# A chunk-state scan put wholly on VectorE and spread over more turns, its output stage packed into fewer

## The chip, the cores and the metric

The kernel runs on one core of a Trainium2 chip. The core has five engines with a queue of instructions each: TensorE (PE in the rows, its weight loads PEld), VectorE (DVE), ScalarE (ACT), GpSimd (POOL) and SyncE (SP), which here only issues DMA transfers. The metric is the device time of one execution in microseconds; several executions are timed and the median is taken.

## The reference

One decoder layer works on x of 1024 tokens by 2048 channels, in float32. A normed x goes through one projection of 2048 by 4096 columns, whose parts are a pooling branch, its gate, a state-space branch `u` and its gate. The state-space branch is what the change touches: 64 groups of 16 channels, each with a complex state of 64, and a linear recurrence over time.

```
bu = einsum(u, bb)                       # per group
s[t] = a * s[t-1] + bu[t]                # complex, associative scan over 1024 tokens
y = Re(c s) + d * u
g = gelu(y)
hg = g @ w_glu
yb = hg[:, :1024] * sigmoid(hg[:, 1024:]) * silu(ssm_gate)
h = x + concat(ya, yb) @ w_out           # ya: pooling branch
out = rmsnorm(h + (p @ w_ple) * sigmoid(h @ w_ple_gate))
```

GELU is computed as y * sigmoid(c0 * (y + 0.044715 y^3)) with c0 = 1.5958.

## The kernel before, in words

The program is a list of **steps**. Nearly all of them are matmul steps of the large projections. One step of the input projection is 12 matmuls of 128x512: two weight blocks, three products each (every float32 weight and input is split into two fp32r parts, and hi*hi, hi*lo and lo*hi are taken), for both halves of the tokens. Before a step runs, its weight block, loaded from HBM into a tile `raw`, is split: ACT casts it into the first half of a tile `w` (L210), DVE subtracts to get the second half (L99, `w<-raw,w`). `emit(s)` writes these splits up to `SA = 4` steps ahead of the matmuls, and there are six `w` tiles. After the last step of a block of eight, a "gate post" reads two finished PSUM banks: two multiplies of 128x512 on DVE, two sigmoids on ACT, two more multiplies on DVE.

**Turns.** The state-space branch is a Python generator, `ssm()`, that is advanced in the background: `emit` calls `next` on it once for each 2.56 us of nominal matmul time, which for the steps here is once per step. What the generator issues up to its next `yield` is one turn. So a turn lies between two groups of 12 matmuls, on every engine in program order, and an extra `yield` moves all later state-space work one step of 12 matmuls on.

The branch works on chunks of T = 8 tokens, NC = 128 chunks. Its stages around the change:

- `ss_v`: per turn eight small matmuls give chunk inputs, copied by ACT and DVE into two tiles `V` of 64 chunks each (128 partitions x 64 chunks x 64).
- `ss_scan`: the recurrence over chunks. First eight *bulks*: each multiplies the states of the eight even chunks of 16 by the complex factor AR, AI and adds them to the odd ones, four `tensor_tensor` operations of 128x512 (`t<-V,AR`, `t<-V,AI`, `V<-V,t` twice). Then 63 sequential steps over the odd chunks, each four operations of 128x64 on DVE (`tA`, `tB`, `V`, `V`), two steps per turn. After every eighth step one more bulk fills the even chunks of the 16 just passed. Before, the bulks of odd j in the first stage and all of the second stage are on POOL.
- `ss_y`: for each of 16 sets of four groups (g0), 16 small matmuls (L1005 on `ytm`, `yu`; L1007 on `yl`, `ys`; each stands as several rows), then the GELU, then a store. `shift(g0 + 4)` copies the states for the next set out of V (four ACT and four DVE copies), `mask_t` makes `ytm` from the loaded `yt` on POOL, `ld(g0 + 8)` loads `yt`, `yu` and `yl`, 256 KB each. The first two turns of `ss_y` are taken early, inside the scan.

The scan's stage lies between the last small matmul of `ss_v` and the first of `ss_y`; PE meanwhile runs input-projection steps. The GELU result goes to `g_d` in HBM, and is loaded again (`gt`) by steps that have a fixed place in the list.

Of the kernel before, what the change touches and what calls it, by code (L numbers as in the profile page):

```python
# [11 lines left out]
AF = mybir.ActivationFunctionType  # L12
ALU = mybir.AluOpType
# [3 lines left out]
P = 128  # L17
# [22 lines left out]
def hybrid_trunk(ctx: ExitStack, tc: tile.TileContext, x, p, norm_gain, w_in, w_pool, pool_scale,  # L40
# [4 lines left out]
    dve = nc.vector  # L45
    act = nc.scalar
    pool = nc.gpsimd
# [4 lines left out]
    out = out[0]  # L52
# [33 lines left out]
    def st(dt=F32, shape=(P, HT), name="st"):  # L86
        return st_p.tile(list(shape), dt, tag="st", name=name)
# [4 lines left out]
    def aux(name="aux"):  # L92
        return aux_p.tile([P, HT], F32, tag="aux", name=name)
# [4 lines left out]
    def tt(eng, o, a, b, op):  # L98
        eng.tensor_tensor(out=o, in0=a, in1=b, op=op)  # L99

    def ts(eng, o, a, s1, op0, s2=None, op1=None):
        if op1 is None:
            eng.tensor_scalar(out=o, in0=a, scalar1=s1, scalar2=None, op0=op0)
        else:
            eng.tensor_scalar(out=o, in0=a, scalar1=s1, scalar2=s2, op0=op0, op1=op1)

    def stt(o, a, s, b, op0, op1):
        dve.scalar_tensor_tensor(out=o, in0=a, scalar=s, in1=b, op0=op0, op1=op1)
# [16 lines left out]
    AR = cst.tile([P, 64], F32, name="AR")  # L125
# [47 lines left out]
    def store(o, i, n=1):  # L173

        late.append([n, o, i])
# [359 lines left out]
    for h in range(2):  # L535
        for c0 in range(0, KD, 4):
# [7 lines left out]
            for kk, mb in chs:  # L544
                k = c0 + kk
# [31 lines left out]
    def both(*gens):  # L577
        gens = list(gens)
        while gens:
            gens = [g for g in gens if next(g, "end") != "end"]  # L580
            yield
# [276 lines left out]
    V = {}  # L858

    def u_rows(dst, g0):  # L860
        sp.dma_start(out=dst.rearrange("p (g k) -> p g k", g=4),
                     in_=u_d.rearrange("(g c) t k -> (c t) g k", c=C)[:, g0:g0 + 4])
# [39 lines left out]
    def cmul(eng, cur, prev, ar, ai, t1, t2):  # L902

        tt(eng, t1, prev, ar, ALU.mult)
        n = len(prev.shape)
        a, b = ("p (r c) -> p r c", 1) if n == 2 else ("p k (r c) -> p k r c", 2)
        sw = prev.rearrange(a, r=2)
        sw = sw[:, ::-1] if n == 2 else sw[:, :, ::-1]
        tt(eng, t2.rearrange(a, r=2), sw, ai.rearrange(a, r=2), ALU.mult)
        tt(eng, cur, cur, t1, ALU.add)  # L910
        tt(eng, cur, cur, t2, ALU.add)

    def bulk(eng, cur, prev):
        n = cur.shape[1]
        t1 = st(name="t1")[:, 0:n * 64].rearrange("p (k c) -> p k c", c=64)
        t2 = st(name="t2")[:, 0:n * 64].rearrange("p (k c) -> p k c", c=64)
        cmul(eng, cur, prev, AR.unsqueeze(1).to_broadcast([P, n, 64]),
             AI.unsqueeze(1).to_broadcast([P, n, 64]), t1, t2)

    def ss_scan():  # L920

        for j in range(8):
            v = V[j // 4][:, (j % 4) * 16:(j % 4) * 16 + 16]
            bulk(pool if j % 2 else dve, v[:, 1::2], v[:, 0::2])
            yield
        yield
        for k in range(3, NC, 2):
            prev = V[(k - 2) // 64][:, (k - 2) % 64]
            cur = V[k // 64][:, k % 64]
            cmul(dve, cur, prev, AR2, AI2, tA, tB)  # L930
            if k % 16 == 15:
                a = k - 15
                v = V[a // 64]
                a %= 64
                if a:
                    bulk(pool, v[:, a:a + 16:2], v[:, a - 1:a + 14:2])
                else:
                    bulk(pool, v[:, 2:16:2], v[:, 1:14:2])
                    if k > 64:
                        bulk(pool, v[:, 0:1], V[0][:, 63:64])  # L940
            if k % 4 == 3:
                yield
        yield

    def ss_y():
        tiles = {}

        def ld(g0):
            if g0 >= G:
                return  # L950
            ttl, ut, lt = (st(name=nm) for nm in ("yt", "yu", "yl"))

            kr = K_d[g0 * C * P:]
            sp.dma_start(out=ttl.rearrange("p (g m) -> p g m", g=4),
                         in_=bass.AP(tensor=kr.tensor, offset=kr.offset,
                                     ap=[[C, P], [C * P, 4], [1, P]]))
            u_rows(ut, g0)
            sp.dma_start(out=lt.rearrange("p (g m) -> p g m", g=4), in_=L_d[:, g0:g0 + 4])
            tiles[g0] = [lt, ttl, ut]

        def mask_t(g0):
            if g0 >= G:
                return
            tm = st(name="ytm")
            tt(pool, tm.rearrange("p (g c i) -> p g i c", g=4, i=T),
               tiles[g0][1].rearrange("p (g i c) -> p g i c", g=4, i=T),
               mask.unsqueeze(1).unsqueeze(3).to_broadcast([P, 4, T, C]), ALU.mult)
            tiles[g0][1] = tm

        def shift(g0):  # L970
            if g0 >= G:
                return
            sv = st(name="ys")
            tiles[g0].append(sv)
            sv = sv.rearrange("p (c e k) -> p e c k", c=2, e=2)
            c = g0 // 2
            n = 0
            for e in range(2):
                dve.memset(sv[:, e, :, 0:1], 0.0)
                for r in range(2):  # L980
                    for hf in range(2):
                        w = 64 - hf
                        o = sv[r * 64:r * 64 + 64, e, :, hf * 64 + 1:hf * 64 + 1 + w]
                        i = V[hf][e * 64:e * 64 + 64, 0:w, r * 32 + c:r * 32 + c + 2]
                        i = i.rearrange("p k c -> p c k")
                        if n % 2:
                            dve.tensor_copy(out=o, in_=i)
                        else:
                            act.copy(out=o, in_=i)
                        n += 1  # L990

        ld(0)
        yield
        mask_t(0)
        ld(4)
        yield
        shift(0)
        yield
        c0 = 1.5957691216057308
        for g0 in range(0, G, 4):  # L1000
            lt, ttl, ut, sv = tiles.pop(g0)
            b = aux()
            for i in range(4):
                o = b[:, i * P:(i + 1) * P]
                pe.matmul(out=o, lhsT=ttl[:, i * P:(i + 1) * P], rhs=ut[:, i * P:(i + 1) * P],  # L1005
                          start=True, stop=False)
                pe.matmul(out=o, lhsT=lt[:, i * P:(i + 1) * P], rhs=sv[:, i * P:(i + 1) * P],  # L1007
                          start=False, stop=True)
            del lt, ttl, ut, sv
            shift(g0 + 4)  # L1010
            q = st(name="yq")
            act.activation(out=q, in_=b, func=AF.Square)
            ts(dve, q, q, c0 * 0.044715, ALU.mult, c0, ALU.add)
            tt(dve, q, q, b, ALU.mult)
            act.activation(out=q, in_=q, func=AF.Sigmoid)
            tt(dve, q, q, b, ALU.mult)
            store(g_d.rearrange("(g c) t k -> (c t) g k", c=C)[:, g0:g0 + 4],
                  q.rearrange("p (g k) -> p g k", g=4))
            del q
            yield  # L1020
            mask_t(g0 + 4)
            ld(g0 + 8)
            yield

    bg_ssm = [1]

    def ssm():
        yield from ss_prep()
        yield from both(ss_b(), ss_l())
        yield  # L1030
        yield from ss_v()
        y = ss_y()
        for i, _ in enumerate(ss_scan()):
            if i in (20, 22):
                next(y)
            yield
        yield from y
        bg_ssm.clear()

    steps[S0]["pre"].append(lambda: bg.append(ssm()))  # L1040


# [209 lines left out]
    for n in range(2):  # L1252
        for cg in range(4):
# [4 lines left out]
            for at, c, h in ((0, 0, 0), (4, 0, 1), (6, 1, 1), (10, 1, 0)):  # L1258
                for b in range(2):
                    i = max(s0 + at + b - 3, units[0][1] - 2)  # L1260
# [188 lines left out]
    for h in range(2):  # L1449
        for cg in range(CG):  # L1450
# [13 lines left out]
            for i in range(4):  # L1464
                k = 4 * cg + i
# [24 lines left out]
    for i in range(4):  # L1490
        k = 4 * cg + i
# [122 lines left out]
```

## Time and profile before

| | |
|---|---|
| median of three runs | 1747.59 us (1745.96 to 1748.83) |
| the profiled execution's own time | 1748.58 us |
| its span, first to last instruction | 1746.8 us |
| PE busy | 1688.2 us, 97% |
| DVE busy | 1130.8 us, 65% |
| ACT busy | 657.9 us, 38% |
| POOL busy | 349.1 us, 20% |

The median is what counts. The rows come from the profiled execution, whose time is 1.78 us above its span and 0.99 us above the median. An engine's share is an average over the whole span and says little about a stage. In the rows, matmul ends are modelled, so the start of a group is taken as the mark, not its busy time; a few matmul records are missing from the trace, so counts are taken from the program.

### The profile page before, as it was taken

How to read it: one execution, taken by the hardware profiler on the slowest of the kernel's cores; microseconds unless marked ns; L12 is line 12 of the kernel's file. 1: busy time of each engine (PE TensorE's matmuls, PEld its weight loads, DVE VectorE, ACT ScalarE, POOL GpSimd, SP SyncE). 2: the span in 40 equal slices, each digit the busy share in tenths (PEclk: the TensorE clock that was granted, in tenths of full speed). 3: DMA queues.
4: the chain of work that ended last, by engine and by line, in shares of the span. 5: the costliest groups of instructions: out<-in, count | busy, mean ns of one | idle time of the engine just before them, and what ended most of it. 6: DMA issues, size and time to landing. Idle time of an engine off the chain costs nothing.

```text
span 1746.8 us, 22832 instructions
## 1 busy us (share of the span) xinstructions
PE 1688.2 (97%) x7766; PEld 1393.0 (80%) x7766; DVE 1130.8 (65%) x1956; ACT 657.9 (38%) x1379; POOL 349.1 (20%) x379
## 2 busy tenths in 40 slices
PE   8999999999979999999899999999999999999997
PEld 7888877887768888787688778888888787877787
DVE  5754687469996655554967786696574655366642
ACT  6642255351115532332533442252233434344432
POOL 0066234006341104210300000000001332033320
PEclk9999999999999999999999999999999999999999
DMA  8863434452226642577566678694455333363312
GB/s 263 246 179 79 130 116 142 145 171 67 85 67 188 193 145 65 179 226 225 204 235 208 250 234 287 226 343 175 145 182 169 120 122 105 122 213 117 117 56 97
DMA packets 283383, 289.74 MB, mean 166 GB/s; under 512 B 53993, under 2 KB 187138, under 8 KB 282370
## 3 DMA queue, kind: packets, MB, share of 16 engines
q1 hardware_dynamic: 283266, 288.28, 51.0%
q8 instruction: 61, 1.00, 0.2%
q14 instruction: 56, 0.46, 0.1%
HBM read 204.85 MB, written 83.36 MB: 165 GB/s over the span
## 4 chain that ended last, share of the span: by engine, by line
PE 49%; DVE 3%; DMA 2%; issue 2%; ACT 1%; POOL 1%; SPq 0%; ACTq 0%; POOLq 0%; DVEq 0%
PE mm L244 17%; PE mm L232 15%; PE aux L232 7%; PE mm L254 7%; PE aux L244 2%; DVE w L99 1%; PE bk L1351 1%; POOL nat L99 1%; DVE cb L99 1%; DMA cb<-gq_d 1%; DMA cb<-cm_d 1%; DMA wq<-in_w_out_dram 1%; ACT cb L406 0%; DMA sgt<-sg_d 0%; DVE cs L99 0%
## 5 line engine op out<-in xcount | busy, mean ns | idle before, releaser
L254 PE MATMUL mm<-hn,w 128*128 128x512 f32 x3072 | 729.0, 395 | 13.0 <-ACT w L210 5.8
L254 PEld LDWEIGHTS mm<-hn,w 128*128 128x128 f32 x3072 | 575.5, 189 | 136.5 <-DVE w L99 7.9
L99 DVE TENSOR_TENSOR w<-raw,w 128x256 fp32r<-128x256 f32 (+1 forms) x440 | 277.7, 645 | 281.2 <-ACT w L217 147.8
L232 PE MATMUL mm<-cb,w 128*128 128x512 f32 x1440 | 334.3, 390 | 7.7 <-DVE w L99 4.7
L244 PE MATMUL mm<-w,h 128*128 128x512 f32 x1359 | 320.1, 392 | 6.1 <-DVE w L99 6.1
L232 PEld LDWEIGHTS mm<-cb,w 128*128 128x128 f32 x1440 | 269.1, 188 | 68.1 <-DVE w L99 7.8
L244 PEld LDWEIGHTS mm<-w,h 128*128 128x128 f32 x1359 | 252.2, 188 | 60.2 <-DVE w L99 9.0
L210 ACT CAST w<-raw 128x256 fp32r<-128x256 f32 x312 | 121.0, 406 | 246.7 <-PE mm L254 176.4
L200 ACT CAST w<-wq 128x512 fp32r<-128x512 f32 x144 | 89.3, 621 | 206.2 <-PE mm L232 87.3
L217 ACT CAST w<-raw 128x512 fp32r<-128x512 f32 x128 | 79.3, 621 | 209.3 <-PE mm L244 150.5
L99 POOL TENSOR_TENSOR hs<-h 128x512 f32<-128x512 f32 x32 | 51.6, 1639 | 490.9 <-DMA hl<-h_d 452.6
L232 PE MATMUL aux<-cb,w 128*128 128x512 f32 x576 | 135.3, 390 | 2.7 <-ACT w L200 1.4
L232 PEld LDWEIGHTS aux<-cb,w 128*128 128x128 f32 x576 | 107.9, 188 | 26.2 <-DVE w L99 2.2
L99 DVE TENSOR_TENSOR w<-wq,w 128x512 fp32r<-128x512 f32 x144 | 101.1, 702 | 16.9 <-ACT w L200 16.9
L99 POOL TENSOR_TENSOR nat<-nat,fg 128x512 f32<-128x512 f32 x28 | 45.9, 1667 | 237.8 <-ACT sig L1377 210.1
L99 DVE TENSOR_TENSOR xtl<-mm,xtl 128x512 f32<-128x512 f32 x80 | 55.1, 689 | 47.5 <-PE mm L232 47.5
L99 POOL TENSOR_TENSOR pf<-pf 128x1023 f32<-128x1023 f32 (+7 forms) x28 | 45.5, 1624 | 172.3 <-DVE pf L99 160.1
L99 DVE TENSOR_TENSOR cb<-cb 128x512 fp32r<-128x512 f32 x84 | 58.0, 725 | 15.4 <-ACT cb L406 15.4
L406 ACT CAST cb<-cb 128x512 fp32r<-128x512 f32 x84 | 49.0, 619 | 23.9 <-DMA cb<-gq_d 9.5
L504 ACT ACTIVATE gs<-mm 128x512 f32<-128x512 f32 x32 | 18.7, 598 | 92.2 <-DVE mm L99 74.5
L99 POOL TENSOR_TENSOR t<-V,AR 128x512 f32<-128x512 f32 (+2 forms) x13 | 16.7, 1284 | 153.9 <-DMA raw<-in_w_in_dram 96.1
L244 PE MATMUL aux<-w,p 128*128 128x512 f32 x192 | 44.8, 389 | 0.0
(212 smaller groups left out, 1665.7 us busy)
## 6 DMA issues: line engine op xcount, KB each, us to landing
raw<-in_w_in_dram SPq DMA_DIRECT2D x136, 256.0 KB, 3.0
raw<-in_w_ple_gate_dram SPq DMA_DIRECT2D x112, 256.0 KB, 3.2
wq<-in_w_out_dram SPq DMA_DIRECT2D x16, 1024.0 KB, 9.2
h_d<-xtl SPq DMA_DIRECT2D x64, 256.0 KB, 3.1
cb<-cm_d SPq DMA_DIRECT2D x48, 256.0 KB, 5.3
xT_d<-xt SPq DMA_DIRECT2D x32, 256.0 KB, 4.0
wq<-in_w_glu_dram SPq DMA_DIRECT2D x16, 512.0 KB, 7.5
xtl<-xT_d SPq DMA_DIRECT2D x32, 256.0 KB, 5.2
```

What stands on the lines that cost most here:

```text
L99: eng.tensor_tensor(out=o, in0=a, in1=b, op=op)
L200: act.copy(out=w[0], in_=src)
L210: act.copy(out=w[:, 0], in_=raw)
L217: act.copy(out=hi, in_=raw)
L232: pe.matmul(out=banks[key], lhsT=w[wi][:, kp], rhs=a[:, ai], start=bool(new) and n == 0, stop=n == 11, skip_group_check=True)
L244: pe.matmul(out=banks[key][:, part], lhsT=a[:, ai, cols], rhs=b[:, part], start=start and j == 0, stop=stop and j == 2)
L254: pe.matmul(out=banks[key], lhsT=w[:, wi, i], rhs=a[:, ai], start=start and i == 0 and j == 0, stop=stop and i == 1 and j == 2)
L406: act.copy(out=sl[:, 0], in_=f(sl[:, 1]))
L504: act.activation(out=s, in_=b, func=AF.Sigmoid)
L1351: pe.transpose(fin["b"][tb][:, (k % 4) * P:(k % 4 + 1) * P], hs[:, tb * P:(tb + 1) * P], ident)
```

## The change

The change edits the scan and the output stage of the state-space branch, and the two indices at which the output stage's first turns are taken inside the scan.

```diff
-    def bulk(eng, cur, prev):
+    def bulk(cur, prev):
...
-        cmul(eng, cur, prev, AR.unsqueeze(1).to_broadcast([P, n, 64]),
+        cmul(dve, cur, prev, AR.unsqueeze(1).to_broadcast([P, n, 64]),
              AI.unsqueeze(1).to_broadcast([P, n, 64]), t1, t2)
...
         for j in range(8):
             v = V[j // 4][:, (j % 4) * 16:(j % 4) * 16 + 16]
-            bulk(pool if j % 2 else dve, v[:, 1::2], v[:, 0::2])
+            bulk(v[:, 1::2], v[:, 0::2])
             yield
+            if j % 2:
+                yield
...
                 if a:
-                    bulk(pool, v[:, a:a + 16:2], v[:, a - 1:a + 14:2])
+                    bulk(v[:, a:a + 16:2], v[:, a - 1:a + 14:2])
                 else:
-                    bulk(pool, v[:, 2:16:2], v[:, 1:14:2])
+                    bulk(v[:, 2:16:2], v[:, 1:14:2])
                     if k > 64:
-                        bulk(pool, v[:, 0:1], V[0][:, 63:64])
+                        bulk(v[:, 0:1], V[0][:, 63:64])
             if k % 4 == 3:
                 yield
+            if k % 16 == 15:
+                yield
         yield
...
             act.activation(out=q, in_=b, func=AF.Square)
-            ts(dve, q, q, c0 * 0.044715, ALU.mult, c0, ALU.add)
-            tt(dve, q, q, b, ALU.mult)
-            act.activation(out=q, in_=q, func=AF.Sigmoid)
+            stt(q, q, 1 / 0.044715, b, ALU.add, ALU.mult)
+            act.activation(out=q, in_=q, func=AF.Sigmoid, scale=c0 * 0.044715)
             tt(dve, q, q, b, ALU.mult)
...
             mask_t(g0 + 4)
             ld(g0 + 8)
-            yield
+            if g0 % 8 == 0:
+                yield
...
         for i, _ in enumerate(ss_scan()):
-            if i in (20, 22):
+            if i in (31, 34):
                 next(y)
```

The bulks that leave POOL are these. On POOL, in the second stage of the scan before, the two bulks after the first sixteen and the second sixteen chunks stand so (`t` are scratch tiles, `V` the states):

```order
L99 TENSOR_TENSOR t_4250<-V,AR 128x448
L99 TENSOR_TENSOR t_4251<-V,AI 128x448
L99 TENSOR_TENSOR V<-V,t_4250 128x7x64
L99 TENSOR_TENSOR V<-V,t_4251 128x7x64
L99 TENSOR_TENSOR t_4352<-V,AR 128x512
L99 TENSOR_TENSOR t_4353<-V,AI 128x512
L99 TENSOR_TENSOR V<-V,t_4352 128x8x64
L99 TENSOR_TENSOR V<-V,t_4353 128x8x64
```

After the change POOL has none of these. On DVE, the first of them now stands behind the eighth sequential step, ahead of a weight split (`w`) and of a gate post (`mm`, `gs`):

```order
L99 TENSOR_TENSOR tA<-V,AR_129 128x64
L99 TENSOR_TENSOR tB<-V,AI_130 128x64
L99 TENSOR_TENSOR V<-V,tA 128x64
L99 TENSOR_TENSOR V<-V,tB 128x64
L99 TENSOR_TENSOR t_4314<-V,AR 128x448
L99 TENSOR_TENSOR t_4315<-V,AI 128x448
L99 TENSOR_TENSOR V<-V,t_4314 128x7x64
L99 TENSOR_TENSOR V<-V,t_4315 128x7x64
L99 TENSOR_TENSOR w<-raw,w 128x256
L99 TENSOR_TENSOR mm<-mm,rstd 128x512 x2
L99 TENSOR_TENSOR gs<-gs,mm 128x512 x2
```

So four operations were inserted there into DVE's queue, and the empty turn behind them holds one split and no sequential step.

On PE, the output stage before has 24 large matmuls between every two of its sets (the last small matmuls of one set, then the first of the next):

```order
L1007 MATMUL aux<-ys,yl 128x128
L254 MATMUL mm<-hn,w 128x512 x24
L1005 MATMUL aux<-yu,ytm 128x128
L1007 MATMUL aux<-ys,yl 128x128
L254 MATMUL mm<-hn,w 128x512 x24
L1005 MATMUL aux<-yu,ytm 128x128
```

After it, 24 and 12 alternate (the lines are four further down in the changed file):

```order
L254 MATMUL mm<-hn,w 128x512 x24
L1009 MATMUL aux<-yu,ytm 128x128
L1011 MATMUL aux<-ys,yl 128x128
L254 MATMUL mm<-hn,w 128x512 x12
L1009 MATMUL aux<-yu,ytm 128x128
L1011 MATMUL aux<-ys,yl 128x128
```

Seven of the 15 gaps became single. Between `ss_v` and the first set there are now 672 large matmuls where there were 528, and behind the last set 240 where there were 300; no matmul was added or removed.

## Rows read from the trace of the kernel before

**Rows 1.** The page: its head, and TensorE's and the other engines' busy time.

```profile
span 1746.8 us, 22832 instructions
PE 1688.2 (97%) x7766; PEld 1393.0 (80%) x7766; DVE 1130.8 (65%) x1956; ACT 657.9 (38%) x1379; POOL 349.1 (20%) x379
```

**Rows 2.** Timeline of PE, scan to output stage: start, us, work, [idle before, releaser].

```profile
387.56 22.93 PE L254 MATMUL mm<-hn,w 128*128 128x512 f32 x100
413.32 61.95 PE L254 MATMUL mm<-hn,w 128*128 128x512 f32 x272 [2.83 <-DVE w L99]
476.79 22.81 PE L254 MATMUL mm<-hn,w 128*128 128x512 f32 x96 [1.53 <-ACT w L210]
502.23 14.33 PE L254 MATMUL mm<-hn,w 128*128 128x512 f32 x60 [2.62 <-ACT w L210]
516.40 0.38 PE L1005 MATMUL aux<-yu,ytm 128*128 128x128 f32 x2
526.45 0.77 PE L1007 MATMUL aux<-ys,yl 128*128 128x128 f32 x2 [9.67 <-ACT ys L989]
...
529.43 6.57 PE L254 MATMUL mm<-hn,w 128*128 128x512 f32 x24
535.84 0.38 PE L1005 MATMUL aux<-yu,ytm 128*128 128x128 f32 x2
...
537.54 5.70 PE L254 MATMUL mm<-hn,w 128*128 128x512 f32 x24
543.08 0.38 PE L1005 MATMUL aux<-yu,ytm 128*128 128x128 f32 x2
```

**Rows 3.** Timeline of PE behind the last set of the output stage.

```profile
638.90 68.26 PE L254 MATMUL mm<-hn,w 128*128 128x512 f32 x300
707.00 5.60 PE L254 MATMUL mm<-pd,w 128*128 128x512 f32 x24
```

**Rows 4.** Windows: stretch, length, busy PE, PEld, DVE, ACT, POOL, clock, DMA share, GB/s.

```profile
390.00:423.00 33.00, 30.17 (x134) 24.66 (x133) 31.91 (x36) 5.33 (x14) 24.32 (x16) 1.00 0.15 48
423.00:525.00 102.00, 89.51 (x389) 72.16 (x387) 98.44 (x301) 16.99 (x44) 43.60 (x37) 0.98 0.27 83
525.00:640.00 115.00, 113.55 (x619) 98.97 (x620) 72.59 (x187) 58.02 (x133) 18.37 (x15) 0.97 0.62 186
526.40:529.40 3.00, 2.95 (x14) 2.98 (x15) 2.25 (x10) 2.16 (x6) 0.00 (x0) 0.50 0.17 45
```

**Rows 5.** Timeline of DVE and POOL where POOL's last first-stage bulk ends.

```profile
412.94 2.90 POOL L99 TENSOR_TENSOR V<-V,t 128x512 f32<-128x512 f32 x2
...
414.61 1.77 DVE L99 TENSOR_TENSOR t<-V,AR 128x512 f32<-128x512 f32 x1
...
418.91 0.69 DVE L99 TENSOR_TENSOR t<-V,AR 128x512 f32<-128x512 f32 x1
...
421.44 1.09 DVE L99 TENSOR_TENSOR w<-raw,w 128x256 fp32r<-128x256 f32 x3
...
423.11 1.29 DVE L99 TENSOR_TENSOR mm<-mm,rstd 128x512 f32<-128x512 f32 x2
...
425.67 0.42 DVE L99 TENSOR_TENSOR w<-raw,w 128x256 fp32r<-128x256 f32 x1
426.01 0.22 DVE L99 TENSOR_TENSOR tA<-V,AR 128x64 f32<-128x64 f32 x1
...
427.46 0.42 DVE L99 TENSOR_TENSOR w<-raw,w 128x256 fp32r<-128x256 f32 x1
```

**Rows 6.** Output stage: GELU's last multiply, the mask, a load's landing, `g_d`'s first re-load.

```profile
540.38 0.69 DVE L99 TENSOR_TENSOR yq<-yq,aux 128x512 f32<-128x512 f32 x1 [0.70 <-ACT yq L1015]
...
L99 POOL TENSOR_TENSOR ytm<-yt,mask x16: 1137/1199/1362, 460.8 to 627.6; 128x512 f32<-128x512 f32 x16
...
yl<-L_d SPq DMA_DIRECT2D x14, 256.0 KB, 3.7
...
L1151 SPq DMA_DIRECT2D gt<-g_d x16: 523/690/1669, 681.4 to 781.7; - x16
```

## The prediction

> **What bounds the kernel now.** The page comes first: PE is busy 97% of the span [rows 1], so a time can only come out of the 3% in which PE waits, or out of stretches where it runs slowly. The windows then show where the state-space scan lies and who is full there. From 390 to 525 us DVE is busy 31.91 of 33 and 98.44 of 102 us, POOL 24.32 and 43.60, ACT only 5.33 and 16.99, and PE falls behind its usual share [rows 4]. In this stage DVE, not PE, sets the pace. Last, the timeline of PE alone, read by the starts of its groups [rows 2], against a clean stretch of the same steps: 300 matmuls take 707.00 - 638.90 = 68.10 us, 0.227 us each, so a turn of 12 is 2.72 us [rows 3].
>
> Three losses follow from it.
> - Scan: from 387.56 to 516.40, 128.84 us, PE does 528 matmuls, worth 528 x 0.227 = 119.9. Lost: 9.0 us, of which 6.98 are three waits for a weight split, 2.83 + 1.53 + 2.62 [rows 2].
> - First set of the output stage: from 516.40 to 529.43, 13.03 us. A set without waits takes 537.54 - 535.84 = 1.70. Lost: 11.3 us. 9.67 of it is the wait for `ys`, the states shifted out of V, which must wait until the scan is done [rows 2]. In the three microseconds behind this wait the granted clock is 0.50, the lower of the two levels, 1.2 GHz [rows 4].
> - The next 24 matmuls: 535.84 - 529.43 = 6.41, against 543.08 - 537.54 = 5.54 later. Lost: 0.9 us [rows 2].
>
> Together 21.2 us. Behind 535.84 the sets follow each other at an even 7.24 us (543.08 - 535.84), so the output stage itself loses nothing now.
>
> **Why DVE is full.** While POOL's bulk runs, a DVE operation of 128x512 takes 1.77 us, and once POOL has stopped the same one takes 0.69 [rows 5]. What DVE's work would need alone: a bulk 421.44 - 418.91 = 2.53 us, two sequential steps 427.46 - 426.01 = 1.45, a split 426.01 - 425.67 = 0.34, a gate post 425.67 - 423.11 = 2.56 [rows 5]. Over the scan of before (8 + 1 + 32 = 41 turns) that is 4 x 2.53 + 63 x 0.725 + 41 x 0.34 + 5 x 2.56 = 82.5 us; the record is 31.91 + 98.44 = 130.4 [rows 4]. The 48 us between are DVE waiting inside its operations while POOL is busy 67.9.
>
> **The change, part by part.**
> *Bulks to DVE, 12 more turns.* The scan gets 53 turns, 53 x 2.72 = 144 us of PE time. DVE then has 16 x 2.53 = 40.5 for all bulks (two are an eighth shorter, one small one is extra), 45.7 for the steps, 53 x 0.34 = 18.0 for splits and 7 x 2.56 = 17.9 for gate posts: 122 us, 85% of the turns. By stage: in the first, 12 turns are 32.7 us against 8 x 2.53 + 12 x 0.34 + two posts = 29.4; in the second, five turns are 13.6 us against 5.8 + 2.53 + 1.7 + 1.6 = 11.6. The price of a bulk is bounded by 2.53 below and 4 x 1.77 = 7.1 above [rows 5]. I take 2.53: with the bulks gone, POOL has only two `ytm` operations of 1.2 us in the scan [rows 6], so no cover is left for the long form.
>
> Load is not all; bursts count too. The worst turn has two steps, a bulk, a split and a gate post: 1.45 + 2.53 + 0.34 + 2.56 = 6.9 us. A gate post holds DVE until PE has ended a step; from there four further steps are already split (`SA` = 4), 10.9 us. So a burst stays inside the reserve, and the empty turn pays it back. I expect the three waits on `w` to go: 9.0 us.
>
> *The shift of the first set.* Its wait is what remains of DVE's and POOL's lateness when the scan ends. POOL's last bulk is gone, DVE is no longer late, and between the last bulk and `shift(0)` lie three turns (two before), so 11.3 + 0.9 us go, the slow clock with it. What is late next would be the copies of `shift(0)`, and they have a whole turn ahead of the first set.
>
> *The 12 turns themselves* cost no time: each is 12 matmuls that PE does anyway. They are moved, not added. Had PE nothing to do there, each would cost 2.72 us. They push the first set 144 matmuls on; the seven single gaps take 84 back. The last set ends 60 matmuls, 13.6 us, later in the step list. `g_d` is first re-loaded at 681.4, 42.5 us behind 638.90 [rows 3, 6]; 29 remain, enough for a GELU and a store.
>
> *Single gaps in the output stage.* A pair of sets takes 3 x 2.72 + 2 x 1.7 = 11.6 us where it took 14.5. DVE was busy 72.6 and ACT 58.0 of 115 us there [rows 4]; over 93 us the same work is 78% and 62%. DMA goes from a share of 0.62 to about 0.77. The deadlines shrink most. A set's loads go out as the set two earlier ends, and have 3 x 2.72 + 1.7 = 9.9 us; a landing takes 3.7 and the mask 1.2 [rows 6]. Some masks reuse the `ytm` of the set just done, so PE's end, the mask and the next set are in a chain of about 1.2 to 1.4 us, plus whatever a DVE operation holds it up (0.69), inside a single gap of 2.72. SP issues loads and stores in the same relative order; a store of `yq` sits ahead of the next load, but its last multiply ends at 540.38 + 0.69 = 541.07, 3.5 us behind the end of its set at 537.54 [rows 2, 6], while the load behind it needs the next set's end, 4.4 us on. I take a half microsecond in all, with 0 and 7 gaps x 2 us as the bounds.
>
> *GELU.* 16 operations of DVE go, one operation with a scalar and a PSUM operand takes the place of two. The new one is bounded by 0.69 [rows 6] and 1.77 [rows 5]; even the upper bound adds 17 us to a stage where DVE is idle 42. Cost on the path: nothing, hidden under PE's 24 or 12 matmuls. The scale on ACT is part of an operation that stays.
>
> **Sum.** 1748.58 - 21.2 = 1727.4 for an execution like the profiled one; that one lies 0.99 above the median, so 1726.4, and with 0.6 left over in the output stage **1727.0 us**, 1.2% faster.
>
> **Rivals.**
> *A: DVE's recorded time is its real work.* The trace analysis page of the Trainium skill ("Perfetto Trace Analysis", section "Optimizing Scalar/DVE Operations") says that a saturated DVE may give work away to ACT or even GpSimd, which speaks against moving work onto it; the same section adds that the two share an SBUF port, so that it might not help. As a mechanism here: the 130.4 us stay, and 12 x 2.53 + 12 x 0.34 + 2 x 2.56 = 39.6 come on top, 170 us. PE's clean time for the stretch is 141.9 - 20.3 + 12 x 2.72 = 154.2. PE would wait 15.8 instead of 21.2: 1742. The pair 1.77 and 0.69 speaks against it [rows 5]. Chance 5%.
>
> *B, slower: a bulk on DVE is long whatever POOL does.* At 4 x 1.70 = 6.8 us (the starts lie a little closer than the durations), DVE needs 122 - 40.5 + 16 x 6.8 = 190 us in 154: PE waits 36, and the time is 1726.4 + 36 = 1762. It turns slower than before above 5.9 us a bulk, where 81.5 + 16 b passes 154.2 + 21.2. One bulk with POOL idle took 2.53 [rows 5]. Chance 3%.
>
> *C: the output stage waits in its single gaps.* The mask chain or the loads come late by 0.7 us in each of seven gaps: 1731; by 2 us: 1740. For: DMA gets denser, and the margin at some masks is about 1 us. Against: the longest mask was 1.36 us [rows 6]. Chance 9%.
>
> *D: nothing moves, since the waits only change hands.* The scan's PE waits name ACT as well as DVE [rows 2]; if ACT or the weight loads were late by themselves, PE would wait as before: 1747. ACT is busy 17 of 102 us [rows 4]. Chance 3%.
>
> **How the numbers follow.** My forecast, DVE with slack in the scan and an even output stage, has 80%; its own range is 1724 to 1730, the sum with the runs' scatter of 1.5 either way and up to 2 us left over. A measurement of this kernel can tell about 0.2%, 3.5 us, from no change. Faster: forecast, A and C, 94%. Same: D, 3%. Slower: B, 3%. The range for eight in ten takes the forecast and the nearer half of C: 1723.5 to 1733.
>
> **What would show it.** In the profile after: no operation of 128x512 on DVE above 1 us in the scan, DVE at about 85% there, POOL nearly idle; the wait for `ys` and those for `w` gone from PE's list between the last small matmul of `ss_v` and the first set; the clock at 1.00 throughout; sets at 7.24 and 4.5 us in turn. Wrong would be bulks above 2.6 us, a wait of PE for `ytm`, `yu` or `yl`, or a DVE that is still above 95%.

## The result, and the profile after

The changed kernel took 1726.55 us in the median, against 1748.21 for the kernel before on the same chip. The ratio is 0.9867, with a 95% interval of 0.9854 to 0.9881: 1.3% faster, where the forecast was 1.2%. One of the four runs of the changed kernel was disturbed, at 2694.57 us; it is left out of the ratio, and the median of the other three is 1725.38 us.

The profiled execution has a span of 1723.6 us and a time of 1725.38. Its page answers to [rows 1]:

```profile
span 1723.6 us, 22772 instructions
PE 1682.1 (98%) x7766; PEld 1390.3 (81%) x7766; DVE 1108.0 (64%) x1992; ACT 660.3 (38%) x1379; POOL 282.4 (16%) x327
```

DVE got 36 instructions more and is busy 22.8 us less. A part of that is the GELU, which lost 16 operations; but e3 below, which keeps the GELU of before, has 52 instructions more and is still busy 14.7 us less (1116.1 for 1130.8). A sum of work doesn't behave so; a sum of work and of waiting inside instructions does.

The timeline of PE, as in [rows 2, 3]: start, busy us, work, and idle time before in brackets.

```profile
387.21 152.58 PE L254 MATMUL mm<-hn,w 128*128 128x512 f32 x672
539.63 0.38 PE L1009 MATMUL aux<-yu,ytm 128*128 128x128 f32 x2
...
541.33 5.70 PE L254 MATMUL mm<-hn,w 128*128 128x512 f32 x24
546.87 0.38 PE L1009 MATMUL aux<-yu,ytm 128*128 128x128 f32 x2
...
548.57 2.98 PE L254 MATMUL mm<-hn,w 128*128 128x512 f32 x12
551.39 0.38 PE L1009 MATMUL aux<-yu,ytm 128*128 128x128 f32 x2
...
553.09 5.70 PE L254 MATMUL mm<-hn,w 128*128 128x512 f32 x24
...
631.35 54.66 PE L254 MATMUL mm<-hn,w 128*128 128x512 f32 x240
685.85 5.60 PE L254 MATMUL mm<-pd,w 128*128 128x512 f32 x24
```

The scan is one row now: 672 matmuls in 539.63 - 387.21 = 152.4 us, 0.227 us each, the rate of the clean stretch. Nothing is lost there, where 9.0 us were, and the first set takes 541.33 - 539.63 = 1.70 instead of 13.03. A pair of sets takes 553.09 - 541.33 = 11.76 us. The start of the `pd` matmuls, which both programs reach after the same work, moved from 707.00 [rows 3] to 685.85: 21.15 us, where the prediction summed 21.2. Of these, 0.35 us were there when the scan began (387.56 before, 387.21 after), so scan and output stage gave 20.8. The span fell by 23.2. The other 2 us lie behind this mark, where nothing was changed: from it to the end it is 1039.8 us before, 1037.8 after, and 1037.8 to 1040.7 in the eight experiments below, in no order with their edits. So that part is scatter of single executions.

What PE waited for between 300 and 640 us:

```profile
PE aux L886 <- DMA vu<-u_d: 0.3, 1, 0.3
PE aux L1011 <- ACT ys L993: 0.2, 1, 0.2
```

The windows, as in [rows 4] (stretch, length, busy PE, PEld, DVE, ACT, POOL, clock, DMA share, GB/s):

```profile
390.00:423.00 33.00, 33.00 (x147) 27.32 (x146) 30.04 (x55) 7.70 (x20) 0.00 (x0) 1.00 0.21 64
423.00:540.00 117.00, 117.00 (x520) 96.96 (x519) 95.48 (x365) 25.55 (x61) 2.48 (x2) 1.00 0.30 91
540.00:640.00 100.00, 99.81 (x569) 87.13 (x568) 59.51 (x154) 53.90 (x121) 17.07 (x14) 1.00 0.69 205
```

From 390 to 540 us DVE is busy 125.5 of 150 us, 84%, and POOL 2.5. The clock is 1.00 in all of it.

One sign that the prediction named did not come: no operation of 128x512 on DVE above 1 us. The longest on V takes 1.55 us; it runs beside the one `ytm` mask that POOL computes at 476.27 us. PE lost nothing by it.

### The profile page after: what moved, and what is told of

Its sections match the earlier page's. It is cut to its first block, busy times and chain, and to the rows that moved or that the text cites. A ratio compares the mean times of both kernels' runs of the same rounds, so it can differ in the third digit from the quotient of the medians.

```text
span 1723.6 us, 22772 instructions
## 1 busy us (share of the span) xinstructions
PE 1682.1 (98%) x7766; PEld 1390.3 (81%) x7766; DVE 1108.0 (64%) x1992; ACT 660.3 (38%) x1379; POOL 282.4 (16%) x327
## 4 chain that ended last, share of the span: by engine, by line
PE 50%; DVE 3%; DMA 2%; issue 2%; ACT 1%; POOL 1%; ACTq 0%; POOLq 0%; SPq 0%; DVEq 0%
PE mm L244 18%; PE mm L232 16%; PE aux L232 7%; PE mm L254 7%; PE aux L244 2%; DVE w L99 1%; PE bk L1355 1%; DVE cb L99 1%; DMA cb<-gq_d 1%; POOL nat L99 1%; DMA cb<-cm_d 1%; DMA wq<-in_w_out_dram 0%; ACT cb L406 0%; DMA sgt<-sg_d 0%; DVE wq L99 0%
## 5 line engine op out<-in xcount | busy, mean ns | idle before, releaser
L99 DVE TENSOR_TENSOR w<-raw,w 128x256 fp32r<-128x256 f32 (+1 forms) x440 | 272.4, 632 | 277.4 <-ACT w L217 147.5
L99 POOL TENSOR_TENSOR ytm<-yt,mask 128x512 f32<-128x512 f32 x16 | 19.6, 1222 | 306.2 <-DMA yl<-L_d 178.3
L99 DVE TENSOR_TENSOR sig<-aux,sig 128x512 f32<-128x512 f32 (+1 forms) x33 | 22.0, 668 | 31.2 <-ACT sig L1371 20.8
```

## The experiments

The theory of the prediction (theory 1): DVE paced the scan, since POOL's bulks stretched its operations; the bulks leave POOL, the turns give DVE room, and the single gaps and the GELU give nothing. Its main rivals: the turns alone do it (theory 2), or a good part comes from the denser output stage (theory 2 of e3 and e4). The numbers of the theories are those of each run's own expectation. Each kernel ran in several rounds beside the kernel before, which had medians of 1749.29 in the first four and 1749.91 in the last four; the ratio is to that. For the change itself it is 0.9867.

| run | what it is | median us | ratio, 95% interval |
|---|---|---|---|
| e1 | before, all bulks on DVE | 1731.6 | 0.9902 (0.9889 to 0.9916) |
| e2 | the change, bulks back on POOL | 1726.09 | 0.9871 (0.9856 to 0.9886) |
| e3 | before, with the whole change to the scan | 1728.42 | 0.9884 (0.9870 to 0.9897) |
| e4 | before, with the change to the output stage | 1750.9 | 1.0007 (0.9998 to 1.0016) |
| e5 | the change, all gaps single | 1735.85 | 0.9922 (0.9910 to 0.9934) |
| e6 | the change, POOL reads for nothing | 1734.68 | 0.9917 (0.9904 to 0.9929) |
| e7 | the change, POOL writes for nothing | 1725.68 | 0.9870 (0.9858 to 0.9883) |
| e9 | the change, four empty turns further ahead | 1721.76 | 0.9843 (0.9830 to 0.9856) |

### e1: the move of the engine alone

```diff
-            bulk(pool if j % 2 else dve, v[:, 1::2], v[:, 0::2])
+            bulk(v[:, 1::2], v[:, 0::2])
...
-                    bulk(pool, v[:, a:a + 16:2], v[:, a - 1:a + 14:2])
+                    bulk(v[:, a:a + 16:2], v[:, a - 1:a + 14:2])
```

The other bulks of the second stage likewise; the turns and the output stage are as before.

> All bulks on DVE, but the 12 extra turns taken back and the output stage as before: the move of the engine alone. Theory 1 (POOL's bulks stretch DVE's operations, and only DVE's lateness holds PE): DVE needs 16 x 2.53 + 45.7 + 41 x 0.34 + 5 x 2.56 = 113 us in 41 turns of 2.72 = 112 us, so it is full without slack, but the reserve of four split steps covers a lateness of about 4 us; no operation of 128x512 on DVE above 1 us, the wait for ys 0 to 4 us instead of 9.7, time 1727 to 1732 us. Theory 2 (the extra turns are what pays, the engine is nearly indifferent): DVE at 100% without slack is late again, waits for w and ys of 10 to 20 us, time 1737 to 1748 us.

PE's one wait between 380 and 660 us in e1, and then the window of the scan:

```profile
PE aux L1007 <- ACT ys L989: 2.2, 1, 2.2
```

```profile
390.00:540.00 150.00, 147.72 (x676) 123.24 (x675) 131.85 (x441) 39.54 (x94) 6.00 (x5) 0.99 0.35 105
```

Theory 1's case: the waits for splits are gone, and of the 9.67 us for `ys` [rows 2] 2.2 are left. The scan has only 41 turns here, and so DVE, busy 114.8 of the 120 us from 390 to 510, comes to its end a little late. No operation of 128x512 on V takes over 0.70 us; one of 128x64 takes 0.97, beside a mask of POOL. By the ratios this one edit gives 0.98% of the change's 1.33%, about three quarters.

### e2: the turns alone

```diff
-            bulk(v[:, 1::2], v[:, 0::2])
+            bulk(pool if j % 2 else dve, v[:, 1::2], v[:, 0::2])
...
-                    bulk(v[:, a:a + 16:2], v[:, a - 1:a + 14:2])
+                    bulk(pool, v[:, a:a + 16:2], v[:, a - 1:a + 14:2])
```

> Bulks divided between DVE and POOL as before, but with the 12 extra turns and the changed output stage: the turns alone. Theory 1 (contention costs DVE about 48 us, whatever the turns): DVE needs 82.5 + 12 x 0.34 + 2 x 2.56 + 48 = 140 us in 53 turns, 144 us, 97%: the operations stay at 1.2 to 1.8 us, but most of the lateness has room; time 1728 to 1738 us, with one or two waits for w of 1 to 3 us left. Theory 2 (the extra turns are what pays): 1726 to 1728 us, like the change. Theory 3 (only the move off POOL pays): the waits stay at 15 us or more, time 1741 to 1748 us.

Two operations of the scan in e2, by tile (minimum, median and maximum in ns, stretch, shapes), then the window of the scan, then PE's timeline there:

```profile
L99 DVE TENSOR_TENSOR tB<-V,AI x63: 212/219/1319, 425.6 to 530.2; 128x64 f32<-128x64 f32 x63
L99 POOL TENSOR_TENSOR V<-V,t x26: 317/1348/1747, 392.8 to 534.0; 128x512 f32<-128x512 f32 x20, 128x448 f32<-128x448 f32 x4, 128x64 f32<-128x64 f32 x2
```

```profile
390.00:540.00 150.00, 150.00 (x672) 124.55 (x671) 140.69 (x365) 31.81 (x78) 69.03 (x54) 1.00 0.27 83
```

```profile
385.72 152.58 PE L254 MATMUL mm<-hn,w 128*128 128x512 f32 x672
538.14 0.38 PE L1009 MATMUL aux<-yu,ytm 128*128 128x128 f32 x2
```

The stretching is all there (a 128x64 operation of DVE takes up to 1.32 us instead of 0.22), POOL is busy 69 us and DVE 140.7 of 150. And yet PE waits nowhere in 672 matmuls. The time is the one that theory 2 named; theory 1 had expected one or two waits to be left, and that was wrong. DVE's load, waiting inside operations included, is 94% of the stage here, and the four split steps in reserve carry PE over every burst. (That the load of the whole stage is not enough to tell, e6 shows.) So the two halves of the scan's change are not two parts of a sum. The move of the engine alone gives 0.98%. The turns alone give 1.29%, which these runs can't tell from the 1.33% of both together: with the turns there, taking the bulks off POOL adds nothing that shows.

### e3 and e4: the scan's change and the output stage's apart

e3 takes the output stage back to what it was, and keeps the scan's 53 turns on DVE; e4 does the opposite.

```diff
 e3
-            stt(q, q, 1 / 0.044715, b, ALU.add, ALU.mult)
-            act.activation(out=q, in_=q, func=AF.Sigmoid, scale=c0 * 0.044715)
+            ts(dve, q, q, c0 * 0.044715, ALU.mult, c0, ALU.add)
+            tt(dve, q, q, b, ALU.mult)
+            act.activation(out=q, in_=q, func=AF.Sigmoid)
...
-            if g0 % 8 == 0:
-                yield
+            yield
```

> The scan of the change (all bulks on DVE, 12 more turns), but the output stage as before (two turns in all 15 gaps, the GELU polynomial in two DVE operations). The last set then ends 144 matmuls, 32.7 us, later in the step list than before the change. Theory 1 (the output stage contributes nothing, the gain is the scan's): 1725 to 1729 us, since g_d's re-load still has some 10 us left behind the last matmul of the last set. Theory 2 (the packing is needed so that the late end does not hold the V tiles or g_d back): a new wait behind the output stage of 3 to 15 us, time 1730 to 1742 us.

> The scan as before (bulks divided between DVE and POOL, 41 turns), the output stage of the change (single gaps, one operation for the polynomial). Theory 1 (the output stage loses nothing before and gains nothing): 1746 to 1750 us, the waits for w and for ys as before. Theory 2 (part of the gain is a shorter output stage): 1735 to 1745 us.

PE's wait in e3 and the end of its output stage (timeline), and then PE's waits in e4:

```profile
PE aux L1011 <- DVE ys L991: 0.6, 1, 0.6
```

```profile
650.34 35.62 PE L254 MATMUL mm<-hn,w 128*128 128x512 f32 x156
685.80 5.60 PE L254 MATMUL mm<-pd,w 128*128 128x512 f32 x24
```

```profile
PE aux L1007 <- ACT ys L989: 9.7, 1, 9.7
PE mm L254 <- DVE w L99: 3.3, 1, 3.3
PE mm L254 <- ACT w L210: 2.6, 1, 2.6
```

e3 reaches the `pd` matmuls at 685.80, the change at 685.85. The last set then has 156 matmuls behind it instead of 240, and nothing waits for its stores even so, though little room is left: the last store to `g_d` goes out at 655.0 us, and the first re-load at 660.2. e4 has the waits of before, and its time; its median is 0.9 us above the expected range, while the kernel before that ran beside it took 1.7 us more than its own earlier median (1749.29 for 1747.59). The edits in the output stage, GELU and gaps, give nothing that these runs can tell; the gain is the scan's.

### e5: how far the gaps can be packed

```diff
             ld(g0 + 8)
-            if g0 % 8 == 0:
-                yield
```

> The changed kernel with one turn in all 15 gaps of the output stage: the margin there. A set then comes every 2.82 + 1.70 = 4.5 us, and a load has 2 x 2.82 + 1.7 = 7.3 us until it is needed instead of 10. Theory 1 (the margin was about a microsecond, as predicted): DMA at a share above 0.85, waits of PE for ytm, yu, yl or ys of 0.5 to 1.5 us in most gaps, 1730 to 1742 us. Theory 2 (the stage still hides): 1724 to 1728 us.

PE's waits between 380 and 660 us in e5, and then the window of its output stage:

```profile
PE aux L1009 <- POOL ytm L99: 5.1, 2, 3.0
```

```profile
540.00:625.00 85.00, 79.94 (x462) 70.22 (x462) 54.65 (x142) 50.35 (x110) 17.12 (x14) 0.96 0.73 217
```

The mask is what comes late, and the chain goes on to SP. Its timeline ahead of the first of the two waits, with POOL's mask and PE's set:

```profile
555.29 0.36 SPq L962 DMA_DIRECT2D yl<-L_d  x1
559.93 0.37 SPq L190 DMA_DIRECT2D raw<-in_w_in_dram  x1
...
561.95 0.56 SPq L958 DMA_DIRECT2D yt<-K_d  x1
...
567.71 1.12 POOL L99 TENSOR_TENSOR ytm<-yt,mask 128x512 f32<-128x512 f32 x1 [7.94 <-DMA yt<-K_d]
...
568.88 0.79 PE L1009 MATMUL aux<-yu,ytm 128*128 128x128 f32 x2 [3.00 <-POOL ytm L99]
```

SP stands for 4.3 us at the load of a weight (`raw`), whose buffer a split of DVE has yet to free; the set's `yt` is issued behind it and three stores at 561.95, and the mask, which waits for `yt` to land, starts 5.8 us later. The second wait, 2.06 us at 610.33, has the same chain: the load of a weight at 602.31, `yt` at 604.31, the mask at 609.15. SP stands there in the change too, as its list of waits for 540 to 640 us shows (total, times, longest), and no set is late:

```profile
SPq L190 <- DVE w L99: 31.3, 12, 6.2
```

So what e5 takes away is the room for such a stand; the stand itself was there. The clock falls to a mean of 0.96 in the window. The `pd` matmuls start at 692.95, 7.1 us behind the change's. Theory 1 had the price and the place, but not the form: two gaps of 15 pay 2 to 3 us each, most pay nothing, and DMA's share stays at 0.73, below what had been expected. This is the rival C of the prediction, one step further on: with half of the gaps single it doesn't happen, with all of them it does.

### e6 and e7: what POOL does to DVE, by itself

Each of the 12 new turns issues work on POOL that nothing uses; the output is untouched. In e6 POOL reads two SBUF operands, in e7 it only writes. (The first diff leaves out the line that makes the tile `dm` and the second call of `dummy`, in the sequential steps; the second diff is against e6, and the comments are added here.)

```diff
+    def dummy():                       # e6
+        for _ in range(16):
+            tt(pool, dm, rstd[:, 0:P], rstd[:, P:2 * P], ALU.mult)
...
             if j % 2:
+                dummy()
                 yield
...
-            tt(pool, dm, rstd[:, 0:P], rstd[:, P:2 * P], ALU.mult)    # e7
+            pool.memset(dm, 0.0)                                      # 32 of them
```

> The changed kernel with work for POOL that nobody needs: in 12 of the scan's turns 16 multiplies of 128x128, which read two finished SBUF tiles and write a tile that nothing reads. The output is untouched. Theory 1 (POOL's reads stretch DVE's operations whatever the data): POOL is busy for 60 us or more in the scan, DVE's 128x512 operations and 128x64 steps are stretched during it, DVE's busy time in the scan grows by 30 to 60 us from about 122, its slack of 22 us is used up, and PE waits again: 1730 to 1750 us. Theory 2 (in the kernel before, DVE's long operations came from the data that it shared with POOL, not from POOL working): DVE as in the change, 1724 to 1728 us.

> The same as the run before, but POOL's unneeded work only writes: 32 fills of 128x128 in each of 12 turns, nothing read. The output is untouched. Theory 1a (only reads by POOL stretch an operation of DVE with two SBUF inputs): DVE's operations as short as in the change, 1724 to 1728 us. Theory 1b (any work of POOL does): as in the run before, 1730 to 1750 us.

The timeline of e6, two sequential steps and the gate post and split beside them:

```profile
476.52 13.69 POOL L99 TENSOR_TENSOR dm<-rstd 128x128 f32<-128x128 f32 x24
...
481.32 1.28 DVE L99 TENSOR_TENSOR mm<-mm,rstd 128x512 f32<-128x512 f32 x2
...
484.22 0.48 DVE L99 TENSOR_TENSOR tA<-V,AR 128x64 f32<-128x64 f32 x1
484.62 0.21 DVE L99 TENSOR_TENSOR tB<-V,AI 128x64 f32<-128x64 f32 x1
484.76 0.48 DVE L99 TENSOR_TENSOR V<-V,tA 128x64 f32<-128x64 f32 x1
485.27 0.51 DVE L99 TENSOR_TENSOR V<-V,tB 128x64 f32<-128x64 f32 x1
...
487.31 0.41 DVE L99 TENSOR_TENSOR w<-raw,w 128x256 fp32r<-128x256 f32 x1
```

The two steps took 1.45 us with POOL idle [rows 5] and take 487.31 - 484.22 = 3.09 here. The gate post's multiplies, with one operand in PSUM, take 1.28 us for two, as they did with POOL idle (1.29, [rows 5]). One by one they take at most 0.70 us in the scan of before, of the change, of e2 and of e6, whatever POOL does beside them.

The window from 470 to 515 us, of e6, of e7, and then e7's operations on `tA` by tile:

```profile
470.00:515.00 45.00, 43.93 (x194) 36.04 (x192) 43.77 (x112) 5.46 (x13) 34.88 (x65) 1.00 0.30 91
```

```profile
470.00:515.00 45.00, 45.00 (x200) 37.28 (x199) 40.31 (x162) 8.49 (x20) 27.53 (x129) 1.00 0.41 127
```

```profile
L99 DVE TENSOR_TENSOR tA<-V,AR x63: 215/221/227, 424.0 to 531.8; 128x64 f32<-128x64 f32 x63
```

In e6 DVE is busy 43.8 of 45 us and gets 112 instructions done where e7 has 162, and behind this window PE has a new wait of 4.39 us for a split. The wait names ACT, and ACT's timeline tells whose lateness it is, in e6 and, for the wait of 1.53 us [rows 2], in the kernel before:

```profile
516.71 1.26 ACT L504 ACTIVATE gs<-mm 128x512 f32<-128x512 f32 x2 [18.66 <-DVE mm L99]
517.87 1.92 ACT L210 CAST w<-raw 128x256 fp32r<-128x256 f32 x6
518.32 2.07 PE L254 MATMUL mm<-hn,w 128*128 128x512 f32 x4 [4.39 <-ACT w L210]
```

```profile
475.19 1.25 ACT L504 ACTIVATE gs<-mm 128x512 f32<-128x512 f32 x2 [15.81 <-DVE mm L99]
```

ACT stood idle for 18.66 us at the sigmoids of a gate post, until DVE had come to the post's multiplies; six casts for splits were queued behind, and PE ran out of split steps. Before, ACT stood there for 15.81 and, at 500.63, for 17.61 us, and PE's two waits on ACT's casts came right behind. In the change it stands for 5.5 to 6.3 us, and in e2 for at most 11.36 (at 422.26), without a wait of PE. So PE's waits went with how late DVE came to a gate post, and not with its load over the stage: from 390 to 540 us DVE is busy 134.2 us in e6, less than the 140.7 of e2, but e6's 34.9 us of POOL's work lie close together in 45 us, where those of e2 are spread over the stage.

The `pd` matmuls of e6 start at 691.83, 6.0 us late. In e7 POOL is busy 27.5 of the same 45 us, DVE's longest `tA` is 0.227 us, and the time is the change's. So here it was not that POOL worked, but that it read. (The doses are not quite equal, and the operation is another; but in e7 not one of the 63 `tA` is stretched.) Of a DVE instruction with two SBUF inputs the Trainium skill states that it contends with a GpSimd instruction that reads SBUF, and not with one that only writes it ("SBUF — State Buffer", section "Who interferes with whom"); the traces agree for three of the four operations of a step, with 0.48 and 0.22 us as the pair, and not for `tB`, which keeps its 0.21. The dose of e6 was smaller than planned: nothing holds these multiplies back, many ran before the scan, and 34.9 us fell into it where at least 60 had been expected. The rise of DVE's busy time (8.7 us between 390 and 540) missed its expected 30 to 60 with it.

### e9: the same remedy further ahead

PE also waits where two other background parts run together (`ss_b` and `ss_l`). In the change's list for 200 to 380 us there stand:

```profile
PE aux L757 <- DVE m L99: 3.7, 2, 1.9
```

e9 gives that pair an empty turn after every seventh:

```diff
+        n = 0
...
+            n += 1
+            if len(gens) == 2 and n % 7 == 0:
+                yield
```

> The changed kernel with four empty turns more in the stage ahead of ss_v, where ss_b and ss_l run side by side, DVE is busy 85 to 90% and PE waits twice for DVE's m, 1.91 and 1.74 us, with the clock below 1.00 behind the first. The last set of the output stage ends four turns later. Theory 1 (slack in turns is what counts, there as in the scan): both waits go, 1720 to 1724 us. Theory 2 (those waits are a chain of m and its transposes, which empty turns don't shorten, or the late end of the output stage costs what is gained): 1725 to 1730 us.

The window there, of the change and of e9, and e9's start of the `pd` matmuls:

```profile
230.00:290.00 60.00, 56.35 (x253) 45.89 (x252) 51.87 (x83) 33.60 (x59) 24.59 (x18) 0.97 0.41 137
```

```profile
230.00:290.00 60.00, 60.00 (x280) 49.59 (x279) 47.73 (x82) 32.63 (x59) 24.07 (x18) 1.00 0.39 130
```

```profile
681.04 5.60 PE L254 MATMUL mm<-pd,w 128*128 128x512 f32 x24
```

The wait is gone, PE is busy all of the 60 us, and the mark comes 4.8 us sooner. At 1721.76 us e9 is ahead of both kernels, with an interval of its ratio that does not touch that of e7, which has the change's time and ran beside it.

## Why the prediction was right, and where it was not

**The sum.** 9.0 + 11.3 + 0.9 = 21.2 us at the `pd` mark, where 21.15 were measured; the three terms are gone each at its place, as the scan's single row, the first set's 1.70 us and the 5.70 us of its 24 matmuls show. That the sum came so near is in part luck, since 0.35 us of the 21.15 were gone ahead of the scan. The 0.6 us for the output stage came out as 0.2 of waiting. The time fell by 1.1 us more than the prediction had it, measured against the kernel before on the same chip, 1748.21 - 1726.55 = 21.66 for 1747.59 - 1727.0 = 20.6; this is within the scatter behind the mark.

**DVE's need.** 122 of 144 us, 85%, were worked out from the operations' lengths with POOL idle. Measured were 125.5 of 150, 84%. (The stage from `ss_v` to the first set has 56 steps of 12 matmuls and not 53, since three turns lie around the scan; before, 44 and not 41. The gain does not change by it.) Rival A (170 us) and rival B (6.8 us a bulk) fall with that, and e1, where all bulks run on DVE at 0.69 us an operation, shows it without the turns. Rival D, that ACT is late by itself, falls with the waits, and ACT's idle time ahead of its casts shows why they named it: ACT stood behind DVE's gate post.

**The output stage.** 11.6 us for a pair of sets, 11.76 measured; DMA's share 0.77, 0.69 measured. e3 and e4 show that these edits give nothing that the runs can tell, as the sum had it; e5 shows where rival C begins.

**What it had not seen.** It gave the gain to both halves of the scan's change together: bulks off POOL, so that DVE's operations shorten, and turns, so that there is room. The turns by themselves would have done it all, as far as the runs can tell, and the bulks by themselves about three quarters. So the number came out right with a condition that was not needed. Of the turns the prediction said that without POOL's bulks DVE needs 85% of them. It had not asked what DVE needs with the bulks left there: e2's 140.7 of 150. That still fits, and in e2 the contention cost nothing.

**What stays open.** e6 and e7 show that POOL's reads make DVE's operations longer. e2 shows that this can be harmless, and e6, with less load over the stage, that it need not be. No run here tells how close together such work may lie; PE did not wait where ACT stood at a gate post for 11.36 us, and did where it stood for 15.81. Why in e6 every `tB` keeps its 0.21 us, while the three operations around it take 0.48 to 0.51, no run here tells either, nor why most splits (`w<-raw,w`), whose operands are two tiles in SBUF as well, keep their 0.41 us there.

## What to carry to other kernels

An engine's busy time next to another that reads the same memory can hold waiting as well as work, as DVE's did here: take the length of an operation while the other engine is idle, sum the need from that, and compare it with the length of the stage. Then look at stretches shorter than the stage too: e6 waited with DVE at 89% of the stage, and e2 did not at 94%. Where a background stage sets the pace, try giving it more of the foreground's steps before its work is made faster: here they cost nothing, as the foreground had them to do and the background's end had room behind it (e3 left 156 matmuls there without harm). Then look for the point at which the slack ends, since packing gave nothing on this side of it and cost 9 us beyond: half of the gaps single were free, all of them, in e5, were not.

## What was not expected of the hardware

Whether a DVE operation was stretched depended on what it and POOL read, operation by operation. With two operands in SBUF, the operations of 128x64 took 0.22 us beside an idle or a writing POOL. Beside POOL's 128x128 multiplies three of the four took 0.48 to 0.51, and the fourth (`tB`) stayed at 0.21; beside POOL's bulks, whose own operations take a median of 1.35, `tB` too took up to 1.32. With one operand in PSUM, the gate post's multiplies stayed at 0.70 us or less beside all of them.
